# Every fourth half weight block gets its low part from ScalarE and an adding DMA

## Chip, core and metric

The kernel runs on one core of a Trainium2 chip. The core has five engines that run side by side and meet only at semaphores: TensorE (PE in the profile; its weight loads are PEld), VectorE (DVE), ScalarE (ACT), GpSimd (POOL) and SyncE (SP), and 16 DMA engines that carry what SP, ACT or POOL issue. The metric is the device time of one execution in microseconds (us); smaller is better.

## What is computed

One layer of a bidirectional encoder on a sequence of 256 tokens of width 2048, in float32. Cut to what matters here:

```
xn = rms_norm(x, norm_pre_w)
z  = xn @ w_in                                   # 2048 x 13312
u_lru, g_lru, q, k, v, g_attn, m_lru, m_attn = split(z)
u  = centred_depthwise_conv(u_lru)
y_a = (rg_lru(u, forward) + rg_lru(u, reverse)) * silu(g_lru)
y_b = windowed_gqa(rope(q), rope(k), v, sink) * silu(g_attn)
merged = sigmoid(m_lru) * (y_a @ w_proj_a) + sigmoid(m_attn) * (y_b @ w_proj_b)
x  = x + rms_norm(merged @ w_out, norm_post_w)
```

Nearly all the work is in the products with `w_in`, `w_proj_a`, `w_proj_b` and `w_out`: 152 MB of float32 weights, each read once.

## The kernel before

**High and low parts.** TensorE multiplies in float32r, a shorter float32. To keep float32 accuracy, every operand is cut in two: the high part `h` is the operand cast to float32r, the low part is `l = operand - h`, and a product is the sum of three: h·h, h·l and l·h (`mm3`, lines 155 to 158). For weights, ScalarE casts `wh` (line 115, `cast(h, src)`) and VectorE subtracts to get `wl` (line 116).

**The stream of weights.** `load_plan` lists 152 loads of 1 MB each, a tile `raw` of 128 x 2048. SP fetches load i+3 at the start of step i into a ring of three `raw` buffers (`fetch`, line 144), so load i+3 can't start before everything that reads `raw` i is done. Each step has two half steps, numbered q = 2i + h, and each half has one `wh` and one `wl` of 128 x 1024, from rings of five buffers each (line 151). While TensorE works on half step hs, the other engines cut half hs+4 (`split(hs + 4)`); with five buffers this can begin when TensorE is done with half hs-1. The `wh` and `wl` of half q therefore have about four half steps of TensorE's time from the earliest cast to the first product that reads them.

**Two kinds of steps.** "quad" steps have 12 products of 512 columns in a half (lines 156 to 158); the second of the 12 reads `wl`. "blk" steps (`add_pair`) go in pairs of rows: in a half with h = 0 the wide products on `wh` (line 175) come first, in a half with h = 1 the narrow ones on `wl` (line 177) come first, so that the narrow rows of two halves of a step stand side by side, 16 in a row.

**Three stretches.** Up to about 430 us the blocks `gl`, `ga`, `u` and the `ml` gates are made, and beside them the convolution, the gates and the scans of the LRU run on ScalarE and VectorE, written at fixed half steps (`at(...)`). Then come the attention heads with `q`, `pa`, `ma` and `pb`, and from about 817 us the output product `o`. All engines take their instructions in the order of the program; within a half step the work that is due comes ahead of the split.

**GpSimd** does nothing but a few memsets: those of the convolution's padded tile `upad` (lines 369 and 370) wait for the tile's buffer.

Of the kernel before, what the change touches and what calls it, by code (L numbers as in the profile page):

```python
# [14 lines left out]
F32 = mybir.dt.float32  # L15
F32R = mybir.dt.float32r
AF = mybir.ActivationFunctionType
ALU = mybir.AluOpType
# [19 lines left out]
FIRST = 8  # L38
# [47 lines left out]
def body(ctx, tc, x, xT, wall, wlru, pvec, npost, ident_d, mask_d, rope_d, out):  # L86
    nc = tc.nc
# [26 lines left out]
    def parts_of(h, l, src, cast=nc.scalar.copy):  # L114
        cast(h, src)  # L115
        nc.vector.tensor_tensor(l, src, h.bitcast(F32), ALU.subtract)  # L116
# [21 lines left out]
    raws, parts = {}, {}  # L138
# [7 lines left out]
    def split(q, c=0, w=1024, cast=nc.scalar.copy):  # L146
        i, h = q // 2, q % 2
        if i >= len(plan):
            return
        if c == 0:  # L150
            parts[q] = [ring.tile([P, 1024], F32R, tag=f"w{s}", name=f"w{s}{i}_{h}", bufs=5) for s in "hl"]
        wh, wl = parts[q]
        parts_of(wh[:, c:c + w], wl[:, c:c + w], raws[i][:, h * 1024 + c:h * 1024 + c + w], cast)

    def mm3(ps, wh, wl, xh, xl, start, stop):
        nc.tensor.matmul(ps, wh, xh, start=start, stop=False)  # L156
# [113 lines left out]
    for j in range(4):  # L270
        scale_x(0, j)
        split(j // 2, j % 2 * 512, 512, nc.vector.tensor_copy if j == 0 else nc.scalar.copy)
    for j in range(4):
        scale_x(1, j)
        if j % 2 == 1:
            split(2 + j // 2)
# [481 lines left out]
    for i, (_, half) in enumerate(steps):  # L758
        for h in range(2):
            now[0] = hs = 2 * i + h  # L760
            if h == 0:
                fetch(i + 3)
            if hs in first:
                first.pop(hs)()
            if hs < FIRST:
                split(hs + 4)
            for fn in due.pop(hs, ()):
                fn()
            if hs >= FIRST:
                split(hs + 4)  # L770
            half(h, *parts.pop(hs))
# [71 lines left out]
```

## Time and profile before

| | |
|---|---|
| median of 3 runs | 914.86 us (914.55 to 914.86) |
| the profiled execution, its own time | 914.31 us |
| its span from first to last instruction | 912.5 us |
| granted TensorE clock in it, mean | 0.997 |
| share of the span in which ScalarE / VectorE / GpSimd are busy | 60% / 67% / 0% |
| bytes moved by DMA | 172.18 MB |

The profile is one execution. "Busy" is the time in which an engine had an instruction running. A row of a group reads: source line, engine, operation, what it writes and reads, shapes, count, then the busy time and the mean duration of one in ns, then the time in which the engine sat idle just before such instructions and what ended that idle time. Rows of the timeline read: start in us, length in us, engine, line, operation, out<-in, number of instructions merged in the row, and in brackets the idle time before it.

### The profile page before, as it was taken

The page shows a single profiled execution, that of the slowest core. Times are in us where ns is not written, and L with a number is a line of the kernel's source. Part 1 is how long each engine was busy: PE and PEld are TensorE (multiplying, and loading weights), DVE is VectorE, ACT ScalarE, POOL GpSimd, SP SyncE. Part 2 cuts the span into 40 slices and gives each one's busy share as a digit, 9 for nine tenths or more (in the row PEclk, how much of TensorE's full clock was granted, in tenths as well). Part 3 has the DMA queues.
Part 4 walks back from the last instruction along what each step waited for, and adds up shares of the span by engine and source line. Part 5 has one row for each costly group of instructions (what it writes and reads, how often), then busy time and mean ns, then how long its engine had stood idle before and what let it go on. Part 6 is the DMA issues. An engine that isn't in the chain of part 4 may idle for free.

```text
span 912.5 us, 11845 instructions
## 1 busy us (share of the span) xinstructions
PE 903.0 (99%) x4638; PEld 772.1 (85%) x4638; DVE 610.6 (67%) x841; ACT 551.7 (60%) x775; POOL 1.4 (0%) x23
## 2 busy tenths in 40 slices
PE   9999999999999999999999999999999999999996
PEld 8888888888888888888888888888888888888885
DVE  6897877768676868596755666666654655555554
ACT  7969578685969496949445545454554544444451
POOL 0000000000000000000000000000000000000000
PEclk9999999999999999999999999999999999999998
DMA  9744564545564455536654444444444555558532
GB/s 329 261 180 170 194 254 181 208 142 191 199 216 176 184 180 214 181 136 217 218 190 154 173 166 158 151 172 163 161 167 175 204 191 185 185 191 316 185 139 92
DMA packets 27703, 172.18 MB, mean 189 GB/s; under 512 B 3072, under 2 KB 3968, under 8 KB 8576
## 3 DMA queue, kind: packets, MB, share of 16 engines
q1 hardware_dynamic: 26928, 170.27, 51.7%
q10 hardware_dynamic: 720, 1.16, 0.3%
q8 instruction: 36, 0.59, 0.2%
q14 instruction: 19, 0.16, 0.0%
HBM read 169.32 MB, written 2.10 MB: 188 GB/s over the span
## 4 chain that ended last, share of the span: by engine, by line
PE 98%; DMA 1%; DVE 0%; ACT 0%; issue 0%; SPq 0%; DVEq 0%
PE ga L175 6%; PE gl L175 6%; PE u L175 5%; PE o L156 4%; PE o L158 4%; PE o L157 4%; PE ga L177 3%; PE gl L177 3%; PE u L177 3%; PE u_ps L360 2%; PE gate L156 1%; PE gate L158 1%; PE gate L157 1%; PE ma__6163 L156 1%; PE pa__5483 L156 1%; PE ma__5943 L156 1%
## 5 line engine op out<-in xcount | busy, mean ns | idle before, releaser
L116 DVE TENSOR_TENSOR wl<-raw,wh 128x1024 fp32r<-128x1024 f32 (+1 forms) x306 | 370.5, 1215 | 265.0 <-ACT wh L115 264.1
L115 ACT CAST wh<-raw 128x1024 fp32r<-128x1024 f32 (+1 forms) x305 | 315.5, 1045 | 212.1 <-PE o L158 37.0
L175 PE MATMUL gl<-xn,wh 128*128 128x512 f32 x256 | 62.5, 391 | 0.0
L175 PE MATMUL ga<-xn,wh 128*128 128x512 f32 x256 | 62.5, 391 | 0.0
L175 PEld LDWEIGHTS gl<-xn,wh 128*128 128x128 f32 x256 | 46.8, 188 | 9.0
L175 PEld LDWEIGHTS ga<-xn,wh 128*128 128x128 f32 x256 | 46.8, 188 | 9.0
L156 PE MATMUL o<-wh,ms 128*128 128x512 f32 x128 | 49.9, 390 | 0.0
L158 PE MATMUL o<-wh,ms 128*128 128x512 f32 x128 | 49.8, 389 | 0.0
L157 PE MATMUL o<-wl,ms 128*128 128x512 f32 x128 | 49.8, 389 | 0.0
L175 PE MATMUL u<-xn,wh 128*128 128x512 f32 x192 | 46.8, 391 | 0.0
L175 PEld LDWEIGHTS u<-xn,wh 128*128 128x128 f32 x192 | 35.3, 188 | 6.8
L617 ACT ACTIVATE p<-p,nm 128x256 f32<-128x256 f32 x32 | 16.0, 502 | 36.3 <-DVE nm L615 36.3
L177 PEld LDWEIGHTS gl<-xn,wl 128*128 128x128 f32 x256 | 33.0, 191 | 1.3
L177 PEld LDWEIGHTS ga<-xn,wl 128*128 128x128 f32 x256 | 33.0, 191 | 1.3
L177 PE MATMUL ga<-xn,wl 128*128 128x256 f32 x256 | 33.7, 283 | 0.0
L177 PE MATMUL gl<-xn,wl 128*128 128x256 f32 x256 | 33.7, 283 | 0.0
L158 PEld LDWEIGHTS o<-wh,ms 128*128 128x128 f32 x128 | 24.0, 188 | 5.0
L157 PEld LDWEIGHTS o<-wl,ms 128*128 128x128 f32 x128 | 24.0, 188 | 5.0
L156 PEld LDWEIGHTS o<-wh,ms 128*128 128x128 f32 x128 | 24.0, 188 | 4.9
L177 PEld LDWEIGHTS u<-xn,wl 128*128 128x128 f32 x192 | 24.6, 191 | 0.9
L177 PE MATMUL u<-xn,wl 128*128 128x256 f32 x192 | 24.9, 283 | 0.0
L432 DVE SCALAR_TENSOR_TENSOR uu<-upad,pv,uu 128x256 f32<-128x256 f32 x48 | 23.3, 485 | 2.3
(345 smaller groups left out, 2012.7 us busy)
## 6 DMA issues: line engine op xcount, KB each, us to landing
raw<-wall_dram SPq DMA_DIRECT2D x149, 1024.0 KB, 4.8
lraw<-wlru_dram SPq DMA_DIRECT2D x8, 512.0 KB, 5.7
raw<-wall_dram SPq DMA_DIRECT2D x4, 512.0 KB, 7.0
xr<-x_dram SPq DMA_DIRECT2D x4, 512.0 KB, 10.2
raw<-wall_dram SPq DMA_DIRECT2D x4, 256.0 KB, 5.1
xT<-xT_dram SPq DMA_DIRECT2D x4, 256.0 KB, 6.4
np<-npost_dram SPq DMA_DIRECT2D x2, 512.0 KB, 7.7
out_dram<-yw SPq DMA_DIRECT2D x4, 256.0 KB, 2.1
```

Source lines behind the costliest of these rows:

```text
L115: cast(h, src)
L116: nc.vector.tensor_tensor(l, src, h.bitcast(F32), ALU.subtract)
L156: nc.tensor.matmul(ps, wh, xh, start=start, stop=False)
L157: nc.tensor.matmul(ps, wh, xl, start=False, stop=False)
L158: nc.tensor.matmul(ps, wl, xh, start=False, stop=stop)
L175: nc.tensor.matmul(ps, wh[:, sl], a, start=k == 0, stop=k == KT - 1)
L177: nc.tensor.matmul(ps[:, 1], wl[:, sl], a[:, 0], start=False, stop=False)
L360: nc.tensor.matmul(ups[b // 2][:, b % 2, 0], w[:, sl], a[:, m], start=k == 0 and n == 0, stop=k == KT - 1 and n == 2)
L432: nc.vector.scalar_tensor_tensor(u, up[:, j, tap:tap + S], cw[:, tap:tap + 1], u, ALU.mult, ALU.add)
L617: nc.scalar.activation(p[:, t], p[:, t], AF.Exp, bias=nm[:, t:t + 1], accum_out=dn[:, t:t + 1])
```

## The change

```diff
@@ split(q, c, w, cast)
         wh, wl = parts[q]
-        parts_of(wh[:, c:c + w], wl[:, c:c + w], raws[i][:, h * 1024 + c:h * 1024 + c + w], cast)
+        src = raws[i][:, h * 1024 + c:h * 1024 + c + w]
+        if q >= FIRST + 8 and q % 4 == 1:
+            nc.scalar.copy(wh, src)
+            nc.scalar.activation(wl, src, AF.Copy, scale=-1.0)
+            nc.gpsimd.dma_start(wl.bitcast(F32), src, accum_op=ALU.add)
+        else:
+            parts_of(wh[:, c:c + w], wl[:, c:c + w], src, cast)
```

`FIRST` is 8, so the new branch serves q = 17, 21, ... 301: 72 halves, always the second half of an even-numbered load. In these, ScalarE casts as before, then goes over the same 1024 columns once more and writes `wl` = -`src` in float32r, which is -`wh`. A DMA issued by GpSimd then adds `src` to `wl` in SBUF, which leaves `src` - `wh`. VectorE's subtraction is gone for these halves. The source lines below `split` move by six.

On ScalarE, the place where load 32 is cut (its second half is q = 65). `wh` and `wl` are a half's parts; `a`, `gr` and `th` belong to the LRU. Before, and then with the change:

```order
171 L115 CAST wh_0_1820<-raw_1756 128x1024
172 L467 ACT_TABLE_LOAD
173 L467 ACTIVATE a_1811<-gr_1730,cneg 128x256 x2
174 L497 ACTIVATE gr_1730<-a_1811 128x1024
175 L115 CAST wh_1_1847<-raw_1756 128x1024
176 L115 CAST wh_0_1870<-raw_1809 128x1024
177 L498 ACT_TABLE_LOAD
```

```order
183 L115 CAST wh_0_1832<-raw_1768 128x1024
184 L473 ACT_TABLE_LOAD
185 L473 ACTIVATE a_1823<-gr_1741,cneg 128x256 x2
186 L503 ACTIVATE gr_1741<-a_1823 128x1024
187 L155 CAST wh_1_1859<-raw_1768 128x1024
188 L156 ACTIVATE wl_1_1860<-raw_1768 128x1024
189 L115 CAST wh_0_1883<-raw_1821 128x1024
190 L504 ACT_TABLE_LOAD
```

One row is new: the second pass, directly behind the cast of the second half. On VectorE at the same place, before and then with the change:

```order
166 L116 TENSOR_TENSOR wl_0_1821<-raw_1756,wh_0_1820 128x1024
167 L513 TENSOR_TENSOR sg_1814<-sg_1814,sig_1815 128x512
168 L116 TENSOR_TENSOR wl_1_1848<-raw_1756,wh_1_1847 128x1024
169 L471 SCALAR_TENSOR_TENSOR th_1782<-gr_1730,th_1782 128x1024
170 L116 TENSOR_TENSOR wl_0_1871<-raw_1809,wh_0_1870 128x1024
```

```order
154 L116 TENSOR_TENSOR wl_0_1833<-raw_1768,wh_0_1832 128x1024
155 L519 TENSOR_TENSOR sg_1826<-sg_1826,sig_1827 128x512
156 L477 SCALAR_TENSOR_TENSOR th_1794<-gr_1741,th_1794 128x1024
157 L116 TENSOR_TENSOR wl_0_1884<-raw_1821,wh_0_1883 128x1024
158 L116 TENSOR_TENSOR wl_1_1905<-raw_1821,wh_1_1904 128x1024
```

The subtraction for the second half is gone and the rest keeps its order. GpSimd's queue, which held memsets alone, around loads 30 to 40 with the change:

```order
28 L157 DMA wl30_1_1748<-raw30_1650 128x1024
29 L157 DMA wl32_1_1860<-raw32_1768 128x1024
30 L157 DMA wl34_1_1960<-raw34_1880 128x1024
31 L375 MEMSET upad8_2041 128x2x2
32 L376 MEMSET upad8_2041 128x2
33 L157 DMA wl36_1_2071<-raw36_1980 128x1024
34 L157 DMA wl38_1_2200<-raw38_2091 128x1024
35 L157 DMA wl40_1_2311<-raw40_2220 128x1024
```

The 72 new rows stand between the memsets. Each of these DMAs also reads `raw`, so SP's fetch into that buffer, three loads later, now waits for the DMA where it waited for VectorE.

## The prediction

> **What bounds the kernel now.** I read the first page from the top, then TensorE's own waits, then the groups of the two instructions that cut a weight half. The page's busy times and TensorE's granted clock, then the chain that ended last:
>
> ```profile
> span 912.5 us, 11845 instructions
> PE 903.0 (99%) x4638; PEld 772.1 (85%) x4638; DVE 610.6 (67%) x841; ACT 551.7 (60%) x775; POOL 1.4 (0%) x23
> PEclk9999999999999999999999999999999999999998
> PE 98%; DMA 1%; DVE 0%; ACT 0%; issue 0%; SPq 0%; DVEq 0%
> ```
>
> All that TensorE waits for in the whole execution:
>
> ```profile
> PE spin L240 <- POOL eps L235: 1.0, 1, 1.0
> PE u_ps L360 <- ACT wh L115: 0.8, 2, 0.5
> PE kp L583 <- issue: 0.4, 1, 0.4
> ```
>
> TensorE is busy 99% of the span at full clock, and the waits come to 2.2 us. VectorE and ScalarE are faster than they need be, and nothing they give up shortens the span. A change that relieves VectorE can gain at most those 2 us; a change that makes a `wl` late stops TensorE, and a stop of TensorE goes whole into the time. So the question is how late the new `wl` may come.
>
> **Part 1: VectorE loses 72 subtractions, ScalarE gains 72 passes.** The two groups, shapes kept apart:
>
> ```profile
> L115 ACT CAST wh<-raw 128x1024 fp32r<-128x1024 f32 x302 | 313.6, 1049 | 211.0 <-PE o L158 37.0 <-PE pb__6626 L158 13.5 <-PE pb__6940 L158 13.5
> L116 DVE TENSOR_TENSOR wl<-raw,wh 128x1024 fp32r<-128x1024 f32 x302 | 367.8, 1222 | 263.8 <-ACT wh L115 262.9
> ```
>
> VectorE gets rid of 72 x 1.22 = 88 us of busy time. It sat idle 263 us ahead of these very instructions, so most of the 88 us becomes more idle time; value on TensorE's path 0. ScalarE takes 72 passes over 1024 columns. The second pass isn't in the trace, but it has the shape of the cast; two casts in a row take 1.98 us (rows below), so the second adds 0.95 us: 68 us in all, 60% becomes 68%. Whether ScalarE can bear that is a matter of the first stretch, where the LRU runs:
>
> ```profile
> 45.00:450.00 405.00, 404.56 (x2207) 352.11 (x2207) 306.59 (x384) 299.99 (x410) 0.82 (x12) 1.00 0.53 191
> 450.00:730.00 280.00, 280.00 (x1374) 235.77 (x1373) 171.88 (x307) 142.63 (x223) 0.00 (x0) 1.00 0.48 170
> 730.00:900.00 170.00, 169.99 (x764) 140.18 (x763) 91.67 (x95) 70.72 (x82) 0.00 (x0) 1.00 0.52 187
> ```
>
> (Length; busy PE, PEld, DVE, ACT, POOL; clock; share and GB/s of the DMA engines.) There ScalarE is busy 300 of 405 us and gains 33 x 0.95 = 31 us. In the same stretch it waits for VectorE:
>
> ```profile
> ACT uh L115 <- DVE uu L432: 21.0, 7, 4.1
> ACT sig L512 <- DVE sg L190: 20.3, 6, 5.8
> ACT ya L115 <- DVE sg L483: 17.4, 7, 4.2
> ```
>
> These 58.7 us shrink as VectorE loses 33 subtractions there, so what ScalarE gains and what it loses about cancel, and I cost the passes at 0. If that cover were gone, the cast behind a pass would come 0.95 us later.
>
> **Part 2: the new path of a `wl`.** Before: cast, subtraction, product. Now: cast, 0.95 us of second pass, then D, from GpSimd's issue to the moment when TensorE may read. I give the hand-overs 0.05 us, so a `wl` is ready 1.0 + D after its cast. What stands against it is the gap from the end of the cast to the first product that reads `wl`. Four of the 72 places, cast and product; first the first of the tight ones (q = 29) and two of the LRU's period (q = 65, 81):
>
> ```profile
> 86.41 1.98 ACT L115 CAST wh<-raw 128x1024 fp32r<-128x1024 f32 x2
> 90.37 2.08 PE L177 MATMUL ga<-xn,wl 128*128 128x256 f32 x16
> 189.90 1.98 ACT L115 CAST wh<-raw 128x1024 fp32r<-128x1024 f32 x2
> 195.81 2.08 PE L177 MATMUL u<-xn,wl 128*128 128x256 f32 x16
> 238.53 1.98 ACT L115 CAST wh<-raw 128x1024 fp32r<-128x1024 f32 x2
> 244.35 0.39 PE L157 MATMUL ml__2370<-wl,xn 128*128 128x512 f32 x1
> ```
>
> then the last of the tight ones (q = 145), and one of the third stretch (q = 281):
>
> ```profile
> 425.66 1.98 ACT L115 CAST wh<-raw 128x1024 fp32r<-128x1024 f32 x2
> 432.49 0.39 PE L157 MATMUL q__4030<-wl,xn 128*128 128x512 f32 x1
> 831.85 1.05 ACT L115 CAST wh<-raw 128x1024 fp32r<-128x1024 f32 x1 [1.67 <-PE o L158]
> 842.76 0.39 PE L157 MATMUL o<-wl,ms 128*128 128x512 f32 x1
> ```
>
> The first of the two casts in a row is ours and ends 1.05 us after the row's start. In a row of 16 narrow products ours are the ninth to sixteenth, which start 8 x 0.12 us after the row. The gaps are 3.9, 5.8, 4.8, 5.8 and 9.9 us. At 831.85 the cast starts the moment TensorE frees the buffer (ScalarE waited 1.67 us for it), and this is as good as it gets: four half steps of 2.7 us less the cast. In the first stretch ScalarE arrives late, out of a pile of LRU work, and the gap is what is left. So measured, the 39 places after 430 us have gaps of 9.5 to 13.8 us; of the 33 before, twelve lie under 7.0: 3.9, 6.2, 6.4 (at 91, 102 and 114 us), 6.0 (150), 5.8 (197), 4.8 (244), 5.8 (291), 4.8 (339), 5.8 (385), 5.8, 5.9, 5.8 (411, 422, 432).
>
> **D itself the trace does not show:** there is no DMA from SBUF to SBUF in it, none that adds, none issued by GpSimd. The nearest rows, KB each and median us from issue to landing:
>
> ```profile
> raw<-wall_dram SPq DMA_DIRECT2D x149, 1024.0 KB, 4.8
> xr<-x_dram SPq DMA_DIRECT2D x4, 512.0 KB, 10.2
> out_dram<-yw SPq DMA_DIRECT2D x4, 256.0 KB, 2.1
> q1 hardware_dynamic: 26928, 170.27, 51.7%
> ```
>
> The short end is 2.1 us, a store of half the bytes. The long end is 10.2 us, a load of the same 512 KB queued behind others. In between I go by the raw load: an adding DMA reads the 512 KB of `src` and the 512 KB that it adds to, so it moves as many bytes in as a 1 MB load, 4.8 us. The engines are busy 52% of the time with loads, and 1 MB is some 2.9 us of their time (170 MB in 51.7% of 912 us is 361 GB/s), so meeting one at random costs about half of half of that, 0.7 us; and GpSimd must write the descriptors itself, for which I put 0.5 us, a guess between nothing and 1 us. D = 6.0 us.
>
> **The sum.** With D = 6.0 a `wl` needs 7.0 us. The shortfalls of the twelve places are 3.1, 0.8, 0.6, 1.0, 1.2, 2.2, 1.2, 2.2, 1.2, 1.2, 1.1, 1.2 = 17.0 us. Where three follow within 22 us only the largest counts, since ScalarE and VectorE work on while TensorE stands and come out ahead by as much: less 3.8, 13.2 us. The three deep ones (3.9, 4.8, 4.8) lie in piles that part 1 thins on VectorE's side; I take 1 us off each: 10 us. The later stretches: 7.0 is under 9.5, 0 us.
>
> Two more queues. GpSimd's memsets wait 299 us in total for the convolution, which ends such a wait at 206.91 us; with the change that memset stands behind the DMA of q = 81, whose cast ends at 239.6, so it waits for nothing that is not long done, and no DMA stands behind a late memset:
>
> ```profile
> 206.91 0.10 POOL L369 MEMSET upad<- 128x4 f32 x1 [49.06 <-DVE uu L432]
> POOL upad L369 <- DVE uu L432: 299.4, 6, 61.4
> ```
>
> Cost 0. SP's fetch: load i+3 starts when the DMA has landed, 0.1 + 1.0 + 1.0 + 6.0 = 8 us after the cast began, and lands 4.8 us later, at 12.9. Its first cast, five halves on, comes 13.6 us after ours in the third stretch (five half steps of 2.72): just in time. In the first it comes 8.6 to 13 us after, so casts there slip by up to 4 us, but such a load's halves are cut by VectorE alone and are wanted 4 half steps later. I cost it at 0; with D above 7 it eats into those halves too.
>
> 914.3 + 10 = 924.3 for an execution like the profiled one, which is 0.5 us under the median; **925 us** against 914.86.
>
> **The rivals.** *The transfer hides: no change.* If D is 4.8, like the raw load and nothing more, a `wl` needs 5.8 us; only the three deep places fall short, by 1.9, 1.0 and 1.0 us, and VectorE's relief takes most of it: 1 us, 915.8. The point from which it decides is D = 4.9. For it: the rows of 4.8 and 2.1 us. Against it: half of the 72 will meet a load. The Trainium skill has a rule for this: "DMA: Bandwidth & Descriptors", section on the anatomy of a GpSimd DMA, gives about 2.0 us plus bytes over 436 GB/s, and "Collectives: The Full Stack", on the bandwidth ceiling, says that an adding DMA runs at half rate because it reads two sources. By both, as an estimate, D is 2.0 + 2.4 = 4.4 us. The trace agrees with the first for the raw load (4.4 by the rule, 4.8 measured) and shows nothing on the second. By that rule the time would be 915.
>
> *The adding DMA is slow, 8 us or more*, since its read, sum and write may not overlap. D = 8: shortfalls in clusters 32 us less 3, 944. D = 10.2, the long end: 52 us in the first stretch, and after 430 us 23 places fall short by 18.5 us in sum: 985. From D = 8.5 on every stretch pays. For it: nothing in the trace excludes it. Against it: all bytes stay on the chip.
>
> *Faster:* ScalarE and VectorE both get ahead. TensorE's 2.2 us of waits lie ahead of q = 17 or don't depend on them; worth 0.
>
> **How the numbers follow.** Forecast, D from 4.9 to 8, 917 to 944: 0.51. Hidden, up to 916.5: 0.27. Slow, D over 8: 0.20, half of it over 975. Faster by over 0.2%: 0.02. (0.2%, 1.8 us, is about what a measurement of this kernel can tell from no change.) The range is 913.5 to 975: from the hidden case to D near 10, which leaves out about 0.12. Slower 0.71, same 0.27, faster 0.02.
>
> **What the profile after would show.** Right: PE waits for DMA `wl` at 7 to 12 places, all before 435 us, each 0.5 to 2 us; the issue table shows 72 rows of 512 KB at about 6 us; `o` and `pb` have no waits. Wrong: waits of PE on ScalarE's `wh` (the passes cost after all, or the fetch is late), waits after 450 us (D over 8.5), none at all (D under 4.9), or a memset of `upad` that VectorE waits for.

## The result and the profile after

The changed kernel takes **926.1 us** (median of 3, 925.54 to 926.88) against 914.86: ratio 1.0125, 95% interval 1.0102 to 1.0148, slower by 11.2 us. The profiled execution took 926.1 us, 924.3 of them span. Times are medians of fast executions alone, and of the first kernel of experiment 5, whose trace is of a slow one, only the times are used. Its first page, with the DMA queue that GpSimd feeds and the chain that ended last:

```profile
span 924.3 us, 12125 instructions
PE 907.2 (98%) x4638; PEld 771.4 (83%) x4638; DVE 528.6 (57%) x769; ACT 618.2 (67%) x847; POOL 64.2 (7%) x95
...
q0 software_dynamic: 10368, 37.75, 21.4%
...
PE 74%; DMA 13%; issue 8%; DVE 3%; ACT 2%; SPq 0%; DVEq 0%; POOLq 0%; ACTq 0%; POOL 0%
```

The chain was 98% TensorE; now 13% of it is DMA. VectorE lost 82 us of busy time and ScalarE gained 66.5 (88 and 68 counted). TensorE's own waits after (us in total, times, longest):

```profile
PE o L163 <- DMA wl<-raw: 3.4, 3, 1.8
PE gl L183 <- DMA wl<-raw: 1.8, 2, 1.4
...
PE ml__1527 L163 <- DMA wl<-raw: 1.0, 1, 1.0
```

All new waits are for the adding DMA (three more of 0.3 to 0.4 us are left out), and the largest group is `o`, the output product at the very end. The three stretches of the program show the same (length; busy PE, PEld, DVE, ACT, POOL; clock; share and GB/s of the DMA engines):

```profile
45.00:450.00 405.00, 400.55 (x2178) 346.39 (x2177) 263.21 (x343) 328.73 (x442) 30.58 (x46) 1.00 0.73 228
450.00:815.00 365.00, 365.00 (x1758) 305.65 (x1757) 188.68 (x330) 205.63 (x290) 26.05 (x30) 1.00 0.69 218
815.00:905.00 90.00, 86.62 (x380) 69.86 (x379) 34.80 (x41) 45.53 (x55) 6.95 (x8) 1.00 0.84 250
```

TensorE stands for 4.5 us in the first stretch, not at all in the middle, and for 3.4 us in the last 90 us. Idle time alone doesn't give the sum, because the matmul behind each stop loses some 0.1 us as well. So I set the start of the k-th matmul after against the start of the k-th before, and took each place where the distance grows by over 0.12 us:

```
us in the run after   what starts there   later by   total
 91.72                ga (q = 29)          0.28       0.40
103.20                u  (q = 33)          0.25       0.74
114.93                gl (q = 37)          0.51       1.34
163.59                ml (q = 53)          1.13       2.66
247.77                ml (q = 81)          0.42       3.42
295.19                u  (q = 97)          0.48       4.12
354.48                ml (q = 117)         0.54       4.94
392.05                gl (q = 129)         1.60       6.67
840.62                o  (q = 277)         1.91       8.75
874.21                o  (q = 289)         0.48       9.69
885.40                o  (q = 293)         0.18      10.00
897.88                o  (q = 297)         1.46      11.60
```

About **6.7 us** come before 400 us, nothing to speak of from there to 840 us, and **4.9 us** in the output product. The rows shown make up 5.2 and 4.0 us of that; the rest are smaller steps, 0.10 to 0.11 us right behind each stop and 0.2 us each at q = 65 and 113. The issue table (KB each, median us from issue to landing) for the whole run:

```profile
raw<-wall_dram SPq DMA_DIRECT2D x149, 1024.0 KB, 5.0
wl<-raw POOLq DMA_DIRECT2D x72, 512.0 KB, 4.9
...
xr<-x_dram SPq DMA_DIRECT2D x4, 512.0 KB, 13.5
...
np<-npost_dram SPq DMA_DIRECT2D x2, 512.0 KB, 10.8
```

and the adding DMA's row for 45 to 430 us, 430 to 815 us and 815 to 905 us, one after the other:

```profile
wl<-raw POOLq DMA_DIRECT2D x32, 512.0 KB, 5.3
...
wl<-raw POOLq DMA_DIRECT2D x32, 512.0 KB, 4.6
...
wl<-raw POOLq DMA_DIRECT2D x8, 512.0 KB, 9.2
```

Of the 72 issue-to-landing times the least is 4.48 us, the mean 5.88, the largest 11.49; 17 are over 7 us (10 of the first 32, 1 of the next 32, 6 of the last 8). The mean is my 6.0. The mean describes few of them: 29 of the 72 take under 4.6 us, which is what one takes when the DMA engines are free, 26 take 4.6 to 7 us, 4 up to 8 and 13 from there to 11.5 us. Each of the 17 over 7 us has two or more loads in flight beside it; none of the 29 shortest has more than one, and that for at most 1.6 us.

**Why the end of the program is hit.** SyncE's queue between 822 and 853 us (start, length, line, transfer, count):

```profile
822.84 1.06 SPq L144 DMA_DIRECT2D raw<-wall_dram  x2
823.95 0.42 SPq L726 DMA_DIRECT2D np<-npost_dram  x1
824.42 1.06 SPq L730 DMA_DIRECT2D xr<-x_dram  x2
825.53 0.48 SPq L726 DMA_DIRECT2D np<-npost_dram  x1
826.04 0.95 SPq L730 DMA_DIRECT2D xr<-x_dram  x2
840.72 11.84 SPq L144 DMA_DIRECT2D raw<-wall_dram  x4
```

Two weight loads and the six loads of `load_tail`, 5 MB together, are issued within 4.2 us. The next adding DMA is issued at 829.09 into the middle of them. The chain of waits from there on:

```profile
829.09 11.49 DMA wl<-raw
840.62 0.50 PE o L163
...
865.08 9.09 DMA wl<-raw
...
887.60 10.23 DMA wl<-raw
...
897.88 0.50 PE o L163
```

The DMA lands at 840.58. Only then may SP fetch into the buffer that it held: that `raw` load and the one queued behind it go out from 840.72 on, when the next adding DMA goes out too, at 841.09. They share the engines, that DMA takes 10.53 us, holds the fetch until then, and so on: 11.49, 10.53, 7.90, 9.09, 9.25, 10.23. I read this as a chain that the tail loads start and that afterwards keeps itself up without them; experiments 3 and 5 bear on it.

### The profile page after: what moved, and what is told of

It is laid out like the page before. It is cut to its first block, busy times and chain, and to the rows that moved or that the text cites. A ratio compares the mean times of both kernels' runs of the same rounds, so it can differ in the third digit from the quotient of the medians.

```text
span 924.3 us, 12125 instructions
## 1 busy us (share of the span) xinstructions
PE 907.2 (98%) x4638; PEld 771.4 (83%) x4638; DVE 528.6 (57%) x769; ACT 618.2 (67%) x847; POOL 64.2 (7%) x95
## 3 DMA queue, kind: packets, MB, share of 16 engines
q0 software_dynamic: 10368, 37.75, 21.4%
## 4 chain that ended last, share of the span: by engine, by line
PE 74%; DMA 13%; issue 8%; DVE 3%; ACT 2%; SPq 0%; DVEq 0%; POOLq 0%; ACTq 0%; POOL 0%
DMA wl<-raw 9%; DMA raw<-wall_dram 4%; PE ga L181 4%; PE u L181 4%; PE gl L181 4%; PE o L163 2%; PE o L162 2%; PE o L164 2%; PE ga L183 2%; PE u L183 2%; PE gl L183 2%; PE u_ps L366 2%; DVE wl L116 1%; ACT wh L115 1%; PE pa__5066 L162 1%
## 5 line engine op out<-in xcount | busy, mean ns | idle before, releaser
L116 DVE TENSOR_TENSOR wl<-raw,wh 128x1024 fp32r<-128x1024 f32 (+1 forms) x234 | 283.2, 1213 | 295.2 <-ACT wh L115 294.3
L115 ACT CAST wh<-raw 128x1024 fp32r<-128x1024 f32 (+1 forms) x233 | 241.7, 1042 | 152.6 <-DMA raw<-wall_dram 66.0
L157 POOL DMA_DIRECT2D wl<-raw x72 | 62.7, 871 | 835.3 <-ACT wl L156 644.0
L155 ACT CAST wh<-raw 128x1024 fp32r<-128x1024 f32 x72 | 75.5, 1049 | 61.5 <-PE q__4844 L164 4.9
L156 ACT ACTIVATE wl<-raw 128x1024 fp32r<-128x1024 f32 x72 | 76.2, 1058 | 0.0
L116 DVE TENSOR_TENSOR pl<-pt,ph 128x512 fp32r<-128x512 f32 x16 | 11.1, 691 | 43.5 <-ACT ph L115 43.5
L162 PEld LDWEIGHTS o<-wh,ms 128*128 128x128 f32 x128 | 24.0, 188 | 5.1
```

The lines of the kernel that those rows point to most:

```text
L155: nc.scalar.copy(wh, src)
L156: nc.scalar.activation(wl, src, AF.Copy, scale=-1.0)
L157: nc.gpsimd.dma_start(wl.bitcast(F32), src, accum_op=ALU.add)
```

## The experiments

My theory after this: all of the loss hangs on when the adding DMA lands. Rivals: the 72 passes on ScalarE cost it; the traffic slows the loads; the hold on `raw`, not the DMA's own length, makes the late landings. Each edit is against the changed kernel, each ratio against the kernel before.

### 1. The pass without the DMA, with and without VectorE's work

```diff
-            nc.gpsimd.dma_start(wl.bitcast(F32), src, accum_op=ALU.add)
+            nc.vector.tensor_tensor(wl, src, wh.bitcast(F32), ALU.subtract)
```

> The 72 second passes of ScalarE stay, the adding DMA is left out and VectorE subtracts as before, over what the pass wrote. Theory (late wl: TensorE loses time only where it waits for a wl that the DMA completes): the gaps of the tight places bear pass and subtraction, 0.95 + 1.2 us, so 914 to 916 us and no wait of TensorE on a DMA. Rival (the pass: 68 us more on ScalarE make everything late, the DMA is incidental): 920 to 927 us, waits of TensorE on ScalarE or VectorE.

Measured: 925.57 us, ratio 1.0123 (1.0108 to 1.0137). A miss: the passes alone, with VectorE's subtraction kept, cost as much as the whole change. TensorE's waits in this kernel:

```profile
PE kp L589 <- ACT wl L156: 3.1, 1, 3.1
PE gl L183 <- DVE wl L116: 1.7, 2, 1.3
...
PE ga L183 <- DVE wl L116: 1.3, 1, 1.3
```

These are waits for the pass itself (line 156) or for the subtraction of an ordinary half (line 116) that now comes later. About 1.6 of the 11.5 us are a slow spell behind the wait of 3.1 us (last section). Then the DMA line taken out with nothing in its place:

```diff
-            nc.gpsimd.dma_start(wl.bitcast(F32), src, accum_op=ALU.add)
```

> Pass kept, adding DMA left out and nothing in its place: the low part of these 72 halves stays at minus the high part, the sum with the weights is not computed. Theory (late wl): all of the 11 us go, 914 to 916 us, although VectorE is rid of 72 subtractions, since TensorE has no wait to win back. Rival (the pass): 918 us or more. A second rival (VectorE's relief is worth something once the DMA is away): below 912 us.

Measured: 914.59 us, ratio 1.0004 (0.9995 to 1.0014). Beside start-up TensorE has one wait left:

```profile
PE kp L588 <- ACT wl L156: 0.7, 1, 0.7
```

The two together show that the pass isn't free but paid for by VectorE's lost subtraction (in the first kernel that subtraction also stands behind the pass, so its 11 us hold both, the work kept and the longer path). Since pass and relief together cost nothing, all 11 us of the change hang on the DMA.

### 2. The DMA's traffic without its result

```diff
-            nc.scalar.copy(wh, src)
-            nc.scalar.activation(wl, src, AF.Copy, scale=-1.0)
-            nc.gpsimd.dma_start(wl.bitcast(F32), src, accum_op=ALU.add)
+            parts_of(wh, wl, src)
+            nc.gpsimd.dma_start(side, src, accum_op=ALU.add)
...
+    side = const.tile([P, 1024], F32, name="side")
+    nc.gpsimd.memset(side, 0.0)
```

> Cast and subtraction as before, no pass; 72 adding DMAs of the same size read the same halves, but add them to a tile of their own that nobody reads, so only traffic and the hold on the raw buffer are left. (Two small tiles have one buffer in place of two to make room.) Theory (late wl): 914 to 918 us, with raw loads that land later and at most 3 us of it in TensorE's waits. Rival (traffic: 38 MB more on the DMA engines slow the loads and the products whoever waits): 921 us or more.

Measured: 916.95 us, ratio 1.0027 (1.0017 to 1.0036). By 17 us the matmuls are 2.8 us later than before, and from there to the end this doesn't change. The first adding DMA goes out at 42.6 us, so the 2.8 us aren't its traffic; they belong to the start-up, where the extra memset of 0.95 us stands ahead of `eps` and ScalarE's first load goes out 0.9 us later. The waits at the start, and the adding DMA in the issue table:

```profile
PE u_ps L367 <- ACT wh L115: 2.2, 1, 2.2
PE spin L247 <- POOL eps L242: 1.9, 1, 1.9
```

```profile
side<-raw POOLq DMA_DIRECT2D x72, 512.0 KB, 8.6
```

The median landing of 8.6 us is the slowest of all the runs: the DMA goes out as soon as `raw` is there, and most meet two loads or more. Even so, the traffic as such and the `raw` buffers held longer cost nothing where nobody waits for the sum.

### 3. A plain copy in place of the sum

```diff
-            nc.gpsimd.dma_start(wl.bitcast(F32), src, accum_op=ALU.add)
+            nc.gpsimd.dma_start(wl.bitcast(F32), src)
```

> The change, but the DMA copies the weights over what the pass wrote and adds nothing: the low part of these 72 halves is the whole weight. One stream is read in place of two. Theory (the second stream is what the adding DMA costs): the shortest landing falls from 4.5 us after the issue to 3.0 to 3.5, the waits shrink with it, 916 to 920 us. Rival (issue, start and receipt make up the 4.5 us, the added stream is hidden): 4.2 to 4.6 us and 923 to 926.

Measured: 914.78 us, ratio 1.0009 (1.0000 to 1.0017), and TensorE waits for no DMA. Queues and issue table:

```profile
q0 software_dynamic: 10368, 37.75, 10.3%
...
wl<-raw POOLq DMA_DIRECT2D x72, 512.0 KB, 2.9
```

The time is better than expected, and so is the least landing, 2.82 us against 4.48 with the sum: adding costs **1.66 us**. (0.34 of them are GpSimd's issuing instruction, 0.53 us for the copy and 0.87 for the sum.) Same packets and bytes, but the queue takes 10.3% of the engines' time and took 21.4% with the sum. The Trainium skill's "Collectives: The Full Stack", section on the bandwidth ceiling, has the collective that sums at half the rate of the one that copies, because the sum reads two sources. The two rows agree, 21.4 to 10.3.

The shorter transfer also meets fewer loads: the mean landing falls from 5.88 to 3.62 us, and 2 of the 72 are over 7 us in place of 17. These two come at the tail loads, where the chain starts as in the change, but it dies out: 9.64, 7.04, 5.41, 4.54, 2.83. So the chain keeps itself up only with the longer transfer of the sum.

### 4. Issuing the DMA earlier

```diff
-            nc.scalar.copy(wh, src)
             nc.scalar.activation(wl, src, AF.Copy, scale=-1.0)
             nc.gpsimd.dma_start(wl.bitcast(F32), src, accum_op=ALU.add)
+            nc.scalar.copy(wh, src)
```

> The change as it is, but ScalarE writes minus the high part first and casts after it, so the DMA starts 0.95 us earlier and nothing else differs. Theory (late wl): each wait of TensorE shrinks by 0.95 us; of the waits measured with the change (0.3, 0.25, 0.5, 1.1, 0.4, 0.5, 0.5, 1.6 before 400 us, 1.9, 0.5, 0.2, 1.5 in the output product) 0.2, 0.7, 1.0 and 0.5 stay: 917 to 921 us. Rival (the pass) and rival (traffic): 925 to 927 us, since the same work is done.

Measured: 923.26 us, ratio 1.0098 (1.0084 to 1.0111): 2.8 us less than the change, though the two intervals just overlap, and less gained than expected. The rows of the first stretch and of the last:

```profile
wl<-raw POOLq DMA_DIRECT2D x32, 512.0 KB, 5.2
...
wl<-raw POOLq DMA_DIRECT2D x8, 512.0 KB, 9.8
```

The change has 5.3 and 9.2 there: the first stretch is the same, and in the last the DMAs that are issued earlier take longer. Of all 72, 22 now take 8 us or more, where 13 did. Where a DMA collides, the landing is set by the loads, not by the issue. The edit also does one thing that wasn't meant: the cast stands behind the pass, and TensorE has a new wait for it:

```profile
PE kp L589 <- ACT wh L157: 1.0, 1, 1.0
```

### 5. The end of the program

Only the middle, q = 149 to 273:

```diff
-        if q >= FIRST + 8 and q % 4 == 1:
+        if 149 <= q <= 273 and q % 4 == 1:
```

> The change only on q = 149 to 273, the 32 halves between the LRU's work and the output product; all others as before. Theory (what counts is gap against landing, place by place): in that stretch the gaps are 9.5 to 13.8 us and the landings 4.5 to 7.7, so nothing is lost: 914 to 915.5 us. Rival (each adding DMA has its price, 11.3 us over 72 are 0.16 us each): 918 to 920.

Measured: 914.33 us, ratio 1.0002 (0.9993 to 1.0011). So 32 of the 72 cost nothing, and there is no fixed price of 0.16 us for an adding DMA. Then the four `xr` loads, 2 MB, 26 half steps later:

```diff
-                nc.sync.dma_start(xr[t][h], x[t * P:(t + 1) * P, sl])
...
+    at(2 * len(steps) + 28, load_rows)
```

> The change, with the four loads of the residual rows (512 KB each) issued 26 half steps later, at the end of the output product; the two of the norm weights stay. Theory (chain of meetings: an adding DMA that meets several loads lands late, the fetch behind it starts late and two loads run together, which the next adding DMA meets): without the 2 MB the one at 829 us lands within 7.5 us, the following ones within 6.5, and the 4.9 us lost in the output product fall to under 1: 920 to 922 us. Rival (each adding DMA has its own price, the tail loads don't matter): landings of 8 to 11 us there as before and 925 to 927.

Measured: 925.4 us, ratio 1.0119 (1.0106 to 1.0132). A miss in the total. A chain starts without the `xr` loads, at the 1 MB of `np` that stayed: 8.63, 7.28, 7.14, 8.55, 9.27, 10.35. It is shallower at first, and up to 900 us the output product loses 2.3 us where the change loses 4.9. Then the late `xr` loads meet the one adding DMA that is left (10.37 us), and 4 us more go there, 2.3 in the stop and 1.7 in a slow spell behind it (last section). Then only the two halves that meet the tail loads left as before:

```diff
-        if q >= FIRST + 8 and q % 4 == 1:
+        if q >= FIRST + 8 and q % 4 == 1 and q not in (277, 281):
```

> The change on 70 of the 72 halves: q = 277 and 281, the first two whose adding DMA comes while the six tail loads (3 MB) are under way, are cut by VectorE as before. Theory (the tail loads start a chain of meetings that keeps itself up): the chain doesn't start, the five adding DMAs from 852 us on land within 6.5 us as before 815, and the 4.9 us of the output product fall to under 0.5: 920.5 to 922 us. Rival (in the output product adding DMAs meet loads anyway): landings of 8 to 10 us there and 924 to 926.

Measured: 920.56 us, ratio 1.0065 (1.0051 to 1.0078), 5 us better than the change. The last stretch of this kernel, in the issue table and by windows:

```profile
wl<-raw POOLq DMA_DIRECT2D x6, 512.0 KB, 4.5
```

```profile
815.00:905.00 90.00, 90.00 (x402) 74.36 (x401) 39.47 (x44) 44.48 (x53) 5.20 (x6) 1.00 0.72 238
```

The six that remain there take 4.5 to 4.7 us, where the last five of them took 6.3 to 10.2 in the change, and TensorE doesn't stop. So the later links have no cause of their own: without the first two the chain isn't there.

### 6. Is the hold on the buffer the culprit?

Each `raw` cut in two tiles of 1024 columns, the second kind with four buffers, so that SP's fetch of a second half doesn't wait for the latest DMA (loads of 512 KB; two small tiles get one buffer less):

```diff
+        return [ring.tile([P, 1024], F32, tag=f"raw{h}", name=f"raw{i}_{h}", bufs=(3, 4)[h]) for h in range(2)]
...
-        raws[i] = ring.tile([P, 2048], F32, tag="raw", name=f"raw{i}", bufs=3)
-        nc.sync.dma_start(raws[i], wall[i])
+        raws[i] = raw_tiles(i)
+        for h in range(2):
+            nc.sync.dma_start(raws[i][h], wall[i, :, h * 1024:(h + 1) * 1024])
```

> The change, with the raw buffers cut into halves, three for first halves and four for second halves, each half its own load of 512 KB, so no fetch waits for an adding DMA that has just been issued. (Two small tiles have one buffer less to make room.) Theory (chain of meetings): the chain is cut, landings of the 72 mostly 4.5 to 6.5 us, ScalarE's 66 us of waits for raw loads mostly gone, and of the 11 us 2 to 5 stay in the tight places before 400 us: 916 to 920 us. Rival (fixed price): ScalarE's waits go but the time stays, 923 to 927.

Measured: 938.47 us, ratio 1.0258 (1.0231 to 1.0286). A miss in sign: 12 us worse than the change. Landings in its first and last stretch:

```profile
wl<-raw POOLq DMA_DIRECT2D x32, 512.0 KB, 7.3
...
wl<-raw POOLq DMA_DIRECT2D x8, 512.0 KB, 9.6
```

ScalarE no longer waits for `raw` (66.0 us in the change, 2.2 here), but more of the DMAs meet a load: 33 of 72 are over 7 us. So the rival finds no support: with less of a hold the landings get longer. I read it so that the hold makes fetches wait and keeps them off the DMA that frees the buffer. That isn't shown, because the smaller loads are part of this kernel too, and what they do by themselves wasn't tried; the two smaller tiles were in experiment 2 as well, where TensorE lost nothing after start-up.

### 7. The first half in place of the second

```diff
-        if q >= FIRST + 8 and q % 4 == 1:
+        if q >= FIRST + 8 and q % 4 == 0:
```

> The change on q = 20, 24, ... 300, the first halves of the even loads, in place of the second: 71 halves. The buffer is then held by the second half's subtraction 2.7 us later and by the DMA for 2.7 us less, and in the blk steps the wide products come first, so the wl is wanted 1.9 us later. Theory (chain of meetings and late wl): waits before 400 us fall to under 2 us, the output product to under 3: 917 to 921 us. Rival (fixed price of an adding DMA): 924 to 927.

Measured: 925.33 us, ratio 1.0128 (1.0114 to 1.0143), a miss: about the time of the change, by other places. That is the rival's number, but a fixed price is excluded by experiment 5, where 32 halves cost nothing. TensorE's waits:

```profile
PE k__3882 L163 <- DMA wl<-raw: 2.4, 1, 2.4
PE v__660 L163 <- DMA wl<-raw: 1.8, 1, 1.8
```

`o` again (2.8 us in four waits), and in the first stretch two deep places and a few of 0.4 us or less in place of the eight. Choosing the other half doesn't avoid the loss.

## Why the prediction was right in its total and wrong in its parts

Forecast 925.0, measured 926.1. The cause was the one named, a `wl` that lands late. That the total is right to 1.1 us is luck, because two errors cancel: 10 us forecast before 435 us where 6.7 came, 0 forecast in the later stretches where 4.9 came.

- **TensorE bounds, relief is worth nothing: right.** With 88 us of subtractions gone and no wait for the DMA, experiment 1's second kernel takes 914.59 us.
- **Part 1, passes at 0 because ScalarE's waits for VectorE shrink: right, and shown from both sides** by experiment 1. The three waits of 58.7 us are now 22.9:

```profile
ACT sig L518 <- DVE sg L196: 13.3, 6, 5.8
ACT ya L115 <- DVE sg L489: 5.5, 2, 2.8
ACT uh L115 <- DVE uu L438: 4.1, 4, 1.8
```

 The price that I named for a missing cover, 0.95 us per cast, was the right kind of warning: with VectorE's work kept and in the path it was 11 us.
- **Part 2, D = 6.0 us: the mis-sized term.** The mean is 5.88, but I used one number for different cases, and its parts are off: alone it is 4.48 in place of 4.8 + 0.5, and meetings add 1.40 on average in place of 0.7. "Meeting one at random costs about half of half of that, 0.7 us" is the failed sentence: a meeting isn't random and doesn't cost 0.7 us. The fetch waits for the DMA, so loads and DMAs follow each other in a beat; a DMA runs alone at 4.5 us, beside part of a load at 5 to 7, or under whole loads at 8 to 11.5. The hand-overs, which I gave 0.05 us, take 0.40: that is the mean time from the end of the pass to the DMA's issue. So a `wl` whose DMA runs alone is ready 0.95 + 0.40 + 4.5 = 5.9 us after its cast, not 7.0, and a gap of 5.8 us is just about enough.
- **The twelve tight places.** Six of them show in the table of shifts. At ten of the twelve the DMA ran alone or nearly so, in under 4.9 us:

| q | gap before | forecast shortfall | D after | later by |
|---|---|---|---|---|
| 29, 33, 37 | 3.9, 6.2, 6.4 | 3.1, 0.8, 0.6 | 4.56, 6.41, 8.07 | 0.28, 0.25, 0.51 |
| 49, 65 | 6.0, 5.8 | 1.0, 1.2 | 4.54, 4.51 | under 0.12 each |
| 81, 97, 113 | 4.8, 5.8, 4.8 | 2.2, 1.2, 2.2 | 4.50, 4.87, 4.51 | 0.42, 0.48, 0.05 |
| 129 | 5.8 | 1.2 | 4.50 | 1.60 |
| 137, 141, 145 | 5.8, 5.9, 5.8 | 1.2, 1.1, 1.2 | 4.75, 4.74, 4.50 | none |
| 53, 117 (not among the twelve) | 9.9, 8.9 | 0 | 9.09, 8.48 | 1.13, 0.54 |

 Most long landings fell where the gap is wide; at q = 53 and 117 pass, hand-over and landing together were longer still than the gap. The 1 us that I took off each of the three deep places was about right: the gaps there had become 5.6, 5.5 and 5.9 us (q = 29, 81, 113), since ScalarE came 1.8, 0.7 and 1.1 us earlier against TensorE. That, with 5.9 us needed, is why they cost so little. One of the 39 places after 430 us is narrower than I read: the gap at q = 301 is 8.2 us. With 7.0 needed this changes nothing in the sum.
- **The fetch at 0: half wrong.** ScalarE's casts now wait 66 us for `raw`:

```profile
ACT wh L115 <- DMA raw<-wall_dram: 66.0, 31, 5.9
```

 Most of it is hidden, as I said. The largest early step isn't: at q = 129 the DMA took only 4.50 us, but its cast came late. A load that SP issued at 355.94, once the long DMA of q = 117 had landed, meets the next adding DMA (issued 356.37), takes 10.96 us, and ScalarE stands for it (first row); the cast of q = 129 starts at 385.11 where it started at 378.51 before, 1.7 us more than the 4.9 by which everything is late there:

```profile
366.98 1.05 ACT L115 CAST wh<-raw 128x1024 fp32r<-128x1024 f32 x1 [2.20 <-DMA raw<-wall_dram]
...
385.11 1.04 ACT L155 CAST wh<-raw 128x1024 fp32r<-128x1024 f32 x1
```

 My words "with D above 7 it eats into those halves too" describe this; I didn't price it, having D at 6. This is read from the trace and not tried by itself.
- **"The later stretches: 7.0 is under 9.5, 0 us": right for 430 to 815 us, wrong for the end.** Experiment 5 shows both, and waits after 450 us, my sign for a D over 8.5, are there with a D of 7.9 to 11.5, but at the end alone. "`o` and `pb` have no waits" failed for `o`, because I asked what a `wl` needs and not what else is in flight there: the rows of `xr` at 10.2 us, which I quoted as an upper bound, stood for this very place.
- **GpSimd's memsets at 0: right.** In the waits of the changed kernel `upad` no longer appears at all.
- **The rivals.** The hidden case needed D under 4.9, or 4.55 with the hand-over as measured, and alone D is 4.5: such a DMA stands at the very edge. The Trainium skill's two pages gave 4.4 as an estimate, which the trace bears out to 0.1 us for a transfer that meets nothing, though not term by term: adding costs 1.66 us here, and 1.2 in that estimate. Nothing there or in my rival counted the loads. The slow case, 8 us or more, was right for 13 of the 72.

Open: which load decides each of the eight early places, and whether a program with its tail loads far from the adding DMAs, and fetches timed between them, would lose nothing. No version beat the kernel before; experiment 1 shows why, since even a DMA of no length would leave TensorE with nothing to gain.

## What to carry to other kernels

Compare a new latency with the slack place by place, and take it at each place with what is in flight there: alone or under a load, never the mean of both. A transfer that holds a buffer which a fetch waits for can lock into a beat with the fetches; look at what can knock that beat out of step (here a burst of tail loads) before you count the later stretches as safe. And work that is moved to a less loaded engine may be free only together with the relief that comes with it, as here: test the two apart.

## What the runs showed of the hardware

**A stop of TensorE can cost a slow spell on top.** In the kernel with the late `xr` loads TensorE waits over 2 us at the end of the output product:

```profile
903.00 0.39 PE L162 MATMUL o<-wh,ms 128*128 128x512 f32 x1
905.52 0.75 PE L163 MATMUL o<-wl,ms 128*128 128x512 f32 x1 [2.13 <-DMA wl<-raw]
...
908.21 0.63 PE L163 MATMUL o<-wl,ms 128*128 128x512 f32 x1
...
909.28 0.39 PE L163 MATMUL o<-wl,ms 128*128 128x512 f32 x1
```

For some 3.5 us matmuls start 0.43 us apart where they start 0.23 us apart before and after. The windows show the granted clock there:

```profile
905.40:909.50 4.10, 3.98 (x10) 3.14 (x11) 0.00 (x0) 0.00 (x0) 0.00 (x0) 0.58 0.44 179
909.50:913.00 3.50, 3.50 (x17) 2.90 (x16) 0.89 (x3) 0.98 (x3) 0.00 (x0) 1.00 0.00 0
```

The same came behind the 3.1 us wait of `kp` in experiment 1 (0.58 over 4 us, about 1.6 us lost) and behind a wait of 2.1 us in experiment 6 (0.57). It didn't come behind the 1.75 us wait at 840.62 in the change, nor behind the 2.4 us wait of experiment 7 (both 1.00). The Trainium skill's "TensorE: Matmul & The Clock Gate", Part 1, puts the gate behind an idle window of about 3.4 us that runs freely; three of these five stops were enough at 2.1 to 3.1 us, so a stop need not be that long. Length alone doesn't decide either: 2.1 us was enough twice, and 2.4 us once was not.

**An adding DMA of 512 KB inside SBUF**: 4.48 us alone, 2.82 as a copy, 0.87 us of GpSimd's time to issue (0.53 as a copy), and twice a copy's share of the DMA engines (21.4% against 10.3%).
